# Two gate blocks of a latent-attention layer as seven products of halves, and where 32 modulation sums stand

## The chip, the cores and the metric

One core of a Trainium2 chip runs the whole program. TensorE (PE) multiplies, VectorE (DVE), ScalarE (ACT) and GpSimd (POOL) do elementwise work, SyncE's queue (SP) and POOL issue transfers. The metric is the device time of one execution in microseconds (us); smaller is better.

## The reference, cut to what matters

Two layers over a sequence of 512 tokens with 2048 features, all in fp32. Each layer starts with a modulated norm; layer 1 (i = 0) mixes with retention, layer 2 (i = 1) with latent attention.

```python
for i in range(DEPTH):
    mod = (c_act @ ada_w[i] + ada_b[i])[:, None, :]
    shift, scale, gate = jnp.split(mod, 3, axis=-1)
    h = rmsnorm(x, norm_g[i]) * (1.0 + scale) + shift
    ...
    x = x + gate * y
```

```python
def mla_branch(h, ...):
    proj = h @ w_in
    cq, ckv, k_rope, g = jnp.split(proj, [512, 1024, 1088], axis=-1)
    q = rmsnorm(cq, q_norm_g) @ w_uq
    kv = rmsnorm(ckv, kv_norm_g) @ w_ukv
    ...
    o = causal_block_attention(q, k, v)
    return (silu(g) * o) @ w_out
```

The gate g has 2048 columns; the kernel makes it in four blocks of 512. The row of `mod` that is called `gate` takes, for layer 2, 32 sums over 128 x 1024 pieces of `ada_w` (16 for each half of the features); the kernel's names for the halves are (1, 2, 0) and (1, 2, 1).

## The kernel before, in words

Every fp32 product is three products of the fp32r format: each operand is split into a high part (an ACT cast) and a low part (a DVE subtraction), and PE does high by high, high by low, low by high (L163 to L165). So each weight tile of 128 x 1024 costs an ACT cast and a DVE subtraction before PE can use it.

The program up to attention is a list of steps. The main loop takes them in order; for each step it issues the loads on SP, prepares the weights of this step and of `lead` steps ahead, writes the small pieces hung on the step (`beside`), the matmuls, then the modulation sums whose loads the step before asked for (as many as its `rows`), and asks for the next step's. A modulation sum is a DVE instruction with an accumulated output (L1076) on a tile that SP loads into one of two buffers. Each engine works through its own instructions strictly in the order written, PE's weight loads aside.

In order of time: layer 1's projections, some of them in **narrow blocks** (`narrow_steps`: seven products of halves in place of eight, 14 steps of 24 matmuls with 256 columns, so 336 in a block; the program there is L857 to L970); three retention rounds n = 0, 1, 2, in which the output projection (`round_steps`, L1374) is multiplied while the heads of the next pair go through rotation, scores and values; a last round with the block's tail; then layer 2's gate blocks 0 and 1, the query and key/value latents ("c", up to 1625.72 us), **gate blocks 2 and 3** (to 1716.37 us; `g2_steps`: 8 steps of 24 matmuls with 512 columns each, no product saved), and the attention cycles, one for each pair of heads, with the output projection behind.

A narrow block's step names: `b11` (four tiles of one quarter), then for each of two pairs `o`, `a` and `b` steps; `prepare_a` and `prepare_b` first make sums of raw weight halves on DVE (L931 to L935). Its end steps combine seven PSUM banks m1 to m7 into four results: ACT copies, DVE additions (`after_o`, `after_a`, `after_b`).

During gate blocks 2 and 3 three other things happen: the latents are normalised (`latent_norm`, `latent_scale`), each is transposed on PE by 16 transposes (`latent_transposes`, L1755) and split into parts for the attention products (`latent_parts`: qT, kvT); and DVE does the 32 sums of (1, 2, *), two per step.

Of the kernel before, what the change touches and what calls it, by code (L numbers as in the profile page):

```python
# [49 lines left out]
def hybrid_trunk_kernel(  # L50
# [47 lines left out]
    def k4(name, dt=F32R):  # L98
        return base.tile([P, 2, T], dt, tag="k4", bufs=8, name=name)
# [10 lines left out]
    def aux(name):  # L110
        return psum.tile([P, T], F32, tag="aux", bufs=4, name=name)
# [323 lines left out]
    def queued(fn, *args):  # L435
        with behind(A_, V_, T_, S_):
            return fn(*args)
# [848 lines left out]
    def light(block, which, n=1):  # L1286

        for i in which:
            block[i].rows = n
# [126 lines left out]
    for n in range(3):  # L1416
        block = []
        cols = range(4) if n % 2 == 0 else range(3, -1, -1)
        for r, after in zip(cols, [*cols[1:], None]):
            block += round_steps(n, r, go_on(n, r, after))  # L1420
        heads += [retention(2 * n + 2 + i, big) for i in range(2)]
        light(block, (0, 2, 3, 4, 6, 7, 10, 11, 12, 14, 15))
        light(block, (0, 3, 7), 2)
        steps += block


# [152 lines left out]
    for b in range(4):  # L1579
        block[2].beside["multiply"].append(lambda b=b: write_whole(b))  # L1580
        block[3].beside["form"].append(lambda b=b: ACT.copy(o1_banks[3, 2, b], x1_block(b, 2)))
        block[5].beside["form"].append(lambda b=b: seed(3, 0, b))
        block[0].beside["load"].append(lambda b=b: load_residual(3, b, "vr"))
        block[2].beside["load"].append(lambda b=b: load_residual(2, b, "ld"))
        block[5].beside["load"].append(lambda b=b: load_residual(0, b, "vr"))
        block[9].beside["load"].append(lambda b=b: load_residual(1, b, "ld"))
    steps += block
    for h, pieces in enumerate(heads):
        place(pieces, steps, n_p + 16 * (h // 2) + 4 * (h % 2))
# [152 lines left out]
    def latent_scale(n):  # L1742
        for t in range(NT):
            r, v = latent[n, "r"][:, t : t + 1], latent[n][t]
            if t % 2:
                ACT.activation(v, v, AF.Identity, scale=r)
            else:
                DVE.tensor_scalar(out=v, in0=v, scalar1=r, scalar2=None, op0=ALU.mult)

    def latent_transposes(n):  # L1750
        latent[n, "ps"] = []
        for j in range(4):
            ps = aux(f"{n}T_{j}")
            for t in range(NT):
                PE.transpose(ps[:, t * P : (t + 1) * P], latent[n][t][:, j * P : (j + 1) * P], ident)  # L1755
            latent[n, "ps"].append(ps)

    def latent_parts(n, g_c):
        latent[n, "T"] = []
        for j, ps in enumerate(latent[n, "ps"]):  # L1760
            dst = k4(f"{n}T_{j}")
            ACT.activation(dst[:, 0, :], ps, AF.Identity, scale=g_c[:, j : j + 1])
            DVE.scalar_tensor_tensor(
                out=dst[:, 1, :], in0=ps, scalar=g_c[:, j : j + 1], in1=dst[:, 0, :].bitcast(F32),
                op0=ALU.mult, op1=ALU.subtract,
            )
            latent[n, "T"].append(dst)

    wc = w_mla_in[:, 0:1024].rearrange("k (j n) -> k j n", j=2)
    turns2 = turns(  # L1770
        ((lambda: pools["l2"], "bw", 2), (lambda: base, "raw", 3)),
# [3 lines left out]
        "c", lambda kt, j: wc[kt * P : (kt + 1) * P, j, :], lambda n, u, b: form(h2, sums2, n, u, b), *turns2,  # L1775
        latent_rows, lambda second, u: 0,
    )
    g23 = g2_steps(2, rows=lambda u: 2) + g2_steps(3, rows=lambda u: 2)
    for i, n, g_c in ((0, "q", qn_s), (1, "kv", kvn_c)):
        g23[i].beside["form"].append(lambda n=n: latent_norm(n))  # L1780
        g23[i + 1].beside["form"].append(lambda n=n: latent_scale(n))
        g23[2 + 2 * i].beside["multiply"].append(lambda n=n: latent_transposes(n))
        g23[3 + 2 * i].beside["form"].append(lambda n=n, g_c=g_c: latent_parts(n, g_c))
    steps += g23


# [120 lines left out]
    def attend(h):  # L1907
# [72 lines left out]

        return scores, exps, lambda: (queued(reciprocals), queued(normalise)), transposes, split_pt, load_gate, values, result

    def attention_step(pr):

        nx = pr + 1
        here = [attend(2 * pr + s) for s in range(2)] if pr >= 0 else ()
        both = heads2[nx] = {}
        units_ahead()
        if here:
            (sc0, ex0, no0, tr0, sp0, lg0, va0, re0), (sc1, ex1, no1, tr1, sp1, lg1, va1, re1) = here  # L1990
            queued(lg0)
            queued(lg1)
        low = next_unit("ukv")
        if here:
            for i in range(NT):
                queued(sc0, i)
            for i in range(NT):
                queued(ex0, i)
        low()
        if here:  # L2000
            no0()
        queued(uq_products, nx, 2)
        if here:
            for i in range(NT):
                queued(sc1, i)
            for i in range(NT):
                queued(ex1, i)
        t1 = queued(rope_own, both["uq", 2], f"qr_{nx}")
        low = next_unit("ukv") if here else lambda: None
        if here:  # L2010
            no1()
        low()
        for b in range(2):
            queued(uq_products, nx, b)
        sw = queued(rope_swap, both["uq", 2], f"qr_{nx}")
# [12 lines left out]
        queued(rope_lows, t1, both["qr"])  # L2028
        for b in range(2):
            queued(uk_products, nx, b)  # L2030
            low = queued(part_pair, nx, "uk", b)
            low_w = next_unit("uq")
            queued(low)
            low_w()
        if here:
            queued(va0)
            queued(re0)
            queued(tr1)
            for low in [queued(sp1, j) for j in range(3)]:
# [19 lines left out]
    def all_rows():  # L2059
        pieces = [(0, 2, 0), (0, 2, 1), (1, 0, 0)]  # L2060
        yield from later_modulation(pieces, load_c(lpp, "bm", 2), lpp, [("bw", 2)])
        while "l1" not in pools:
            yield None
        l1p = pools["l1"]
        yield from later_modulation([(1, 0, 1), (1, 1, 0), (1, 1, 1)], load_c(l1p, "odd1", 2), l1p, [("odd0", 2)])
        while "l2" not in pools:
            yield None
        yield from later_modulation(
            [(1, 2, n) for n in range(2)], load_c(base, "k4b", 4), pools["l2"], [("bw", 2), ("pt", 4), ("pt", 4)]
        )  # L2070

    later = all_rows()
    loads = [load for step in steps for load, _ in step.units]
# [301 lines left out]
```

## Time and profile before

| | |
|---|---|
| Three runs | 2162.42, 2164.13, 2165.01 us (median 2164.13) |
| Profiled execution | 2164.31 us, its span 2162.5 us |
| PE busy | 2137.0 us, 99% |
| DVE busy | 1641.6 us, 76% |
| ACT busy | 1044.6 us, 48% |
| POOL busy | 103.7 us, 5% |
| DMA | 440.34 MB, mean 204 GB/s |

The profile is of one execution. Times of the trace run from the start of the span. A row of the timeline gives an instruction's start and its length; DVE, ACT and PE instructions overlap at their ends, so the step from one start to the next is a little shorter than a length. An idle time in square brackets is what the engine waited just before, with the engine and line that ended the wait.

### The profile page before, as it was taken

Reading aid. Unit: us, or ns where it says so; the run is one execution under the profiler, and the core shown is the slowest. Engines: PE = TensorE matmul, PEld = TensorE weight load, DVE = VectorE, ACT = ScalarE, POOL = GpSimd, SP = SyncE. Lnnn points to the kernel's source line nnn. Section 1 sums busy time; section 2 is a strip of 40 time slices with the busy share of each in tenths; the row PEclk is TensorE's granted clock in tenths of the full one; section 3 lists DMA queues with packets and bytes.
Section 4 is the critical chain, followed back from the end, with each engine's and each line's share of the span. In section 5 each row is a group of like instructions: output and inputs, shape, how many; then the busy total and the mean of one; then the engine's idle time right before and its main releaser. Section 6 shows DMA issues by size and latency. Waiting matters only on the chain.

```text
span 2162.5 us, 29040 instructions
## 1 busy us (share of the span) xinstructions
PE 2137.0 (99%) x10782; PEld 1814.0 (84%) x10782; DVE 1641.6 (76%) x2411; ACT 1044.6 (48%) x1581; POOL 103.7 (5%) x175
## 2 busy tenths in 40 slices
PE   8999999999999999999999999999999999999997
PEld 6888989898987887888888888898888899888887
DVE  8988878888889788666777777767967777775545
ACT  6767344444444444434344544434444365664443
POOL 0010000010000000000000000010001000000000
PEclk9999999999999999999999999999999999999999
DMA  9975575766668777765646565753458633335333
GB/s 385 384 251 197 191 252 193 232 212 226 223 211 285 243 243 268 233 201 171 222 158 238 170 215 199 245 174 98 169 174 323 239 97 93 101 97 185 113 104 130
DMA packets 204848, 440.34 MB, mean 204 GB/s; under 512 B 19185, under 2 KB 56081, under 8 KB 200865
## 3 DMA queue, kind: packets, MB, share of 16 engines
q1 hardware_dynamic: 192640, 399.57, 55.1%
q0 software_dynamic: 11920, 38.91, 4.7%
q8 instruction: 84, 1.38, 0.3%
q14 instruction: 58, 0.48, 0.1%
q10 hardware_dynamic: 146, 0.01, 0.0%
HBM read 395.42 MB, written 43.00 MB: 203 GB/s over the span
## 4 chain that ended last, share of the span: by engine, by line
PE 85%; DVE 6%; issue 4%; ACT 2%; DMA 2%; POOL 1%; SPq 0%; DVEq 0%; POOLq 0%; ACTq 0%
PE o L1374 14%; PE qk_m L870 7%; PE o L2241 4%; PE x L775 2%; PE y L775 2%; PE y L776 2%; PE y L774 2%; PE x L776 2%; PE x L774 2%; PE s L775 2%; PE s L776 2%; PE s L774 2%; PE qk L412 2%; PE o L165 2%; PE o L164 2%
## 5 line engine op out<-in xcount | busy, mean ns | idle before, releaser
L1374 PE MATMUL o<-o_h,o_whi 128*128 128x512 f32 (+1 forms) x496 | 192.2, 388 | 0.0
L1374 PE MATMUL o<-o_h,o_wlo 128*128 128x512 f32 (+1 forms) x496 | 191.4, 386 | 0.0
L1374 PE MATMUL o<-o_l,o_whi 128*128 128x512 f32 (+1 forms) x496 | 191.3, 386 | 0.0
L138 DVE TENSOR_TENSOR o_wlo<-o_r,o_whi 128x1024 fp32r<-128x1024 f32 x61 | 74.6, 1223 | 49.5 <-ACT o_whi L137 49.4
L1374 PEld LDWEIGHTS o<-o_h,o_wlo 128*128 128x128 f32 x496 | 93.2, 188 | 18.7
L1374 PEld LDWEIGHTS o<-o_h,o_whi 128*128 128x128 f32 x496 | 93.2, 188 | 18.3
L1374 PEld LDWEIGHTS o<-o_l,o_whi 128*128 128x128 f32 x496 | 93.2, 188 | 18.2
L163 PE MATMUL g<-h,g_h 128*128 128x512 f32 x232 | 90.6, 390 | 0.3 <-ACT g_h L137 0.3
L164 PE MATMUL g<-h,g_h 128*128 128x512 f32 x232 | 90.3, 389 | 0.0
L165 PE MATMUL g<-h,g_l 128*128 128x512 f32 x232 | 89.8, 389 | 0.0
L163 PE MATMUL qk<-hT,qk_h 128*128 128x512 f32 x192 | 74.9, 390 | 0.0
L164 PE MATMUL qk<-hT,qk_h 128*128 128x512 f32 x192 | 74.7, 389 | 0.0
L165 PE MATMUL qk<-hT,qk_l 128*128 128x512 f32 x192 | 74.6, 389 | 0.0
L137 ACT CAST o_whi<-o_r 128x1024 fp32r<-128x1024 f32 x61 | 63.5, 1051 | 20.2 <-issue 10.2
L1076 DVE SCALAR_TENSOR_TENSOR mod<-mod,c_odd 128x1024 f32<-128x1024 f32 x48 | 58.5, 1220 | 17.4 <-DMA mod<-in_ada_t_dram 17.4
L353 DVE SCALAR_TENSOR_TENSOR aw<-aw,c_all 128x2048 f32<-128x2048 f32 x30 | 67.5, 2285 | 0.0
L138 DVE TENSOR_TENSOR o_w_lo<-o_w_raw,o_w_hi 128x1024 fp32r<-128x1024 f32 x32 | 39.0, 1220 | 36.9 <-ACT o_w_hi L137 36.9
L138 DVE TENSOR_TENSOR o_l<-o_in,o_h 128x1024 fp32r<-128x1024 f32 x24 | 29.3, 1223 | 48.2 <-ACT o_h L137 48.2
L1076 DVE SCALAR_TENSOR_TENSOR mod<-mod,c_bm 128x1024 f32<-128x1024 f32 x48 | 58.5, 1219 | 4.8 <-DMA mod<-in_ada_t_dram 4.8
L2241 PE MATMUL o<-o_l,o_w_hi 128*128 128x512 f32 (+1 forms) x160 | 55.5, 347 | 0.9 <-DVE o_l L138 0.9
L2241 PE MATMUL o<-o_h,o_w_hi 128*128 128x512 f32 (+1 forms) x160 | 55.7, 348 | 0.2 <-ACT o_h L137 0.2
L2241 PE MATMUL o<-o_h,o_w_lo 128*128 128x512 f32 (+1 forms) x160 | 55.4, 346 | 0.0
(1308 smaller groups left out, 6625.8 us busy)
## 6 DMA issues: line engine op xcount, KB each, us to landing
mod<-in_ada_t_dram SPq DMA_DIRECT2D x128, 512.0 KB, 5.9
o_r<-in_ret_w_out_dram SPq DMA_DIRECT2D x64, 512.0 KB, 4.9
aw<-in_ada_t_dram SPq DMA_DIRECT2D x30, 1024.0 KB, 7.5
g_r<-in_mla_w_in_dram SPq DMA_DIRECT2D x32, 512.0 KB, 4.5
o_w_raw<-in_mla_w_out_dram SPq DMA_DIRECT2D x32, 512.0 KB, 3.8
qk_r<-in_ret_w_in_dram SPq DMA_DIRECT2D x48, 256.0 KB, 3.1
qk_o_r<-in_ret_w_in_dram SPq DMA_DIRECT2D x32, 256.0 KB, 4.3
qk_r<-qk_d SPq DMA_DIRECT2D x32, 256.0 KB, 6.4
```

The source lines that it names most:

```text
L138: DVE.tensor_sub(lo, src, hi.bitcast(F32))
L163: PE.matmul(o, lhs[0], rhs[0], start=first and not seeded, stop=False, skip_group_check=seeded)
L164: PE.matmul(o, lhs[0], rhs[1], start=False, stop=False, skip_group_check=seeded)
L165: return PE.matmul(o, lhs[1], rhs[0], start=False, stop=last, skip_group_check=seeded)
L353: DVE.scalar_tensor_tensor(out=aw, in0=aw, scalar=1.0, in1=c_all, op0=ALU.mult, op1=ALU.mult, accum_out=col,)
L774: PE.matmul(banks[b], a[0], w[0], start=first, stop=False, skip_group_check=True)
L775: PE.matmul(banks[b], a[0], w[1], start=False, stop=False, skip_group_check=True)
L776: PE.matmul(banks[b], a[1], w[0], start=False, stop=True, skip_group_check=True)
L870: PE.matmul(o, p, q, start=first and b + k == 0, stop=k == 2, skip_group_check=True)
L1076: DVE.scalar_tensor_tensor(out=aw, in0=aw, scalar=1.0, in1=silu_c[j], op0=ALU.mult, op1=ALU.mult, accum_out=mc[:, j, b : b + 1],)
L1374: PE.matmul(o, w[i][:, ki, c0 + b * P : c0 + (b + 1) * P], a[j], start=first and i + j == 0, stop=last and i == 1, skip_group_check=True,)
L2241: PE.matmul(banks2[b][:, cols], w[0][i][:, 0, b * P : (b + 1) * P], o2_moving(w, u, cols)[j], start=u + i + j == 0, stop=u == KD - 1 and i ...
```

## The change

Gate blocks 2 and 3 are made by `narrow_steps`, as layer 1's narrow blocks are; `keep` applies Silu in place on ACT and stores through POOL. Their raw tiles come from tags that the loads of that stretch used (`gate_raw`, five turns over two pools). The steps prepare two ahead.

The query latent is transposed one block of 128 at a time in gate block 3's steps (`latent_turn`, `latent_part`), through a single PSUM bank; the key/value latent's 16 transposes and its parts move into the first attention step (`attention_step(-1)`), behind the products that are called `uq_2`.

Of the 32 sums, the 16 of (1, 2, 0) go into the retention rounds: step 8 of each gets one where it had none, steps 10, 11 and 14 two where they had one, so 18 per round instead of 14; steps 8 to 11 of the last block get one each. The 16 of (1, 2, 1) become `row_turn`, two in each attention cycle, with one weight tile `gate_w` for all: each turn is followed on SP's queue by the load of the next tile (`row_load`), which has to wait for that turn.

```diff
-        light(block, (0, 2, 3, 4, 6, 7, 10, 11, 12, 14, 15))
-        light(block, (0, 3, 7), 2)
+        light(block, (0, 2, 3, 4, 6, 7, 8, 10, 11, 12, 14, 15))
+        light(block, (0, 3, 7, 10, 11, 14), 2)
...
+    light(block, (8, 9, 10, 11))
...
-    g23 = g2_steps(2, rows=lambda u: 2) + g2_steps(3, rows=lambda u: 2)
-    for i, n, g_c in ((0, "q", qn_s), (1, "kv", kvn_c)):
...
+    def gate_raw(shape, name):
+        raw_turn[0] += 1
+        pool, tag, bufs = ((pools["l2"], "bw", 2), (base, "raw", 3))[(raw_turn[0] % 5) in (2, 4, 0)]
+        return pool.tile(shape, F32, tag=tag, bufs=bufs, name=f"{name}_r")
...
+        def keep(half, j, c):
+            ACT.activation(c, c, AF.Silu)
...
+        return narrow_steps(
+            f"g2_{gi}", lambda e, j, u0, n: w[e, j][:, u0 : u0 + n, :], lambda n, u: form_half(h2, sums2, n, u),
+            gate_raw, turns2[1], keep,
+        )
...
+    for gi in (2, 3):
+        block = narrow_gates(gi)
+        for step in block[: 13 if gi == 3 else 14]:
+            step.lead = 2
+        for i in (3, 10):
+            block[i].ahead = 2
+        g23 += block
...
-        g23[i + 1].beside["form"].append(lambda n=n: latent_scale(n))
-        g23[2 + 2 * i].beside["multiply"].append(lambda n=n: latent_transposes(n))
-        g23[3 + 2 * i].beside["form"].append(lambda n=n, g_c=g_c: latent_parts(n, g_c))
+        g23[i + 2].beside["form"].append(lambda n=n: latent_scale(n))
+    for j in range(4):
+        g23[14 + 5 + 2 * j].beside["multiply"].append(lambda j=j: latent_turn("q", j))
+        g23[14 + 6 + 2 * j].beside["form"].append(lambda j=j: latent_part("q", qn_s, j, latent["q", "bank"]))
...
+    def row_turn():
...
+        DVE.scalar_tensor_tensor(
+            out=gate_rows["w"], in0=gate_rows["w"], scalar=1.0, in1=gate_rows["c"], op0=ALU.mult, op1=ALU.mult,
+            accum_out=gate_rows["m"][:, j, b : b + 1],
+        )
...
+            row_load(n + 1)
...
+        if pr < 0:
+            for j in range(4):
+                latent["kv", j] = aux(f"kvT_{j}")
+                for t in range(NT):
+                    queued(PE.transpose, latent["kv", j][:, t * P : (t + 1) * P], latent["kv"][t][:, j * P : (j + 1) * P], ident)
...
         low()
+        queued(row_turn)
...
+            if b:
+                queued(row_turn)
             queued(uk_products, nx, b)
```

DVE's order in retention round n = 1, from step 8 to step 9, before (`o_1_1_2_wlo` is the low part of the output weights, `v_0` to `v_3` those of the values that PE multiplies in this step):

```order
L138 TENSOR_TENSOR qk_1_0p<-rope_1_0_t_10407,qk_1_0p 128x512
L138 TENSOR_TENSOR o_1_1_2_wlo_10449<-o_1_1_2_r,o_1_1_2_whi_10448 128x1024
L138 TENSOR_TENSOR v_0_10452<-v_4_r,v_0_10452 128x512
L138 TENSOR_TENSOR v_1_10455<-v_4_r,v_1_10455 128x512
L138 TENSOR_TENSOR v_2_10458<-v_4_r,v_2_10458 128x512
L138 TENSOR_TENSOR v_3_10461<-v_4_r,v_3_10461 128x512
```

and after:

```order
L138 TENSOR_TENSOR qk_1_0p<-rope_1_0_t_10421,qk_1_0p 128x512
L1076 SCALAR_TENSOR_TENSOR mod_1_0_51_10373,mod_1_0_c<-mod_1_0_51_10373,c_odd_8946 128x1024
L138 TENSOR_TENSOR o_1_1_2_wlo_10464<-o_1_1_2_r,o_1_1_2_whi_10463 128x1024
L138 TENSOR_TENSOR v_0_10467<-v_4_r,v_0_10467 128x512
L138 TENSOR_TENSOR v_1_10470<-v_4_r,v_1_10470 128x512
L138 TENSOR_TENSOR v_2_10473<-v_4_r,v_2_10473 128x512
L138 TENSOR_TENSOR v_3_10476<-v_4_r,v_3_10476 128x512
```

One modulation sum now stands ahead of the low part of the weights and of the values.

DVE's order where gate block 2 ends and gate block 3 begins, after (`g_2_m` are PSUM banks of block 2, `g_3_..._l` low parts of block 3's weights; L931 to L935 make the raw sums for the `a` and `b` steps). Before, this place held one low part and two modulation sums for each step:

```order
L875 TENSOR_TENSOR g_3_b_0_l<-g_3_b_0_r,g_3_b_0_h 128x1024
L954 TENSOR_TENSOR g_2_p_14786<-g_2_m_14469,g_2_p_14786 128x512
L955 TENSOR_TENSOR g_2_v<-g_2_p_14786,g_2_p_14822 128x512
L956 TENSOR_TENSOR g_2_v<-g_2_m_14439,g_2_v 128x512
L875 TENSOR_TENSOR g_3_o_l<-g_3_o_r,g_3_o_h 128x1024
L962 TENSOR_TENSOR g_2_p_14786<-g_2_m_14494,g_2_p_14786 128x512
L964 TENSOR_TENSOR g_2_c_14859<-g_2_m_14507,g_2_p_14786 128x512
L966 TENSOR_TENSOR g_2_p_14822<-g_2_p_14786,g_2_p_14822 128x512
L931 TENSOR_TENSOR g_3_o_r<-g_3_o_r,g_3_a_r 128x512
L932 TENSOR_TENSOR g_3_a_r<-g_3_a_r,g_3_b_0_r 128x512
L933 TENSOR_TENSOR g_3_a_r<-g_3_o_r,g_3_b_0_r 128x512
L935 TENSOR_TENSOR g_3_o_r<-g_3_o_r,g_3_a_r 128x512
```

and ACT's order at the same place (L1772 is the Silu in `keep`, L874 the high part of a weight tile):

```order
L1772 ACTIVATE g_2_c_14788<-g_2_c_14788 128x512
L874 CAST g_3_b_0_h<-g_3_b_0_r 128x1024
L953 COPY g_2_p_14822<-g_2_m_14456 128x512
L1772 ACTIVATE g_2_v<-g_2_v 128x512
L874 CAST g_3_o_h<-g_3_o_r 128x1024
L1772 ACTIVATE g_2_c_14859<-g_2_c_14859 128x512
L1772 ACTIVATE g_2_p_14822<-g_2_p_14822 128x512
L874 CAST g_3_a_h<-g_3_a_r 128x1024
```

The combining additions of block 2 now stand between block 3's low parts, and three Silus between its casts.

DVE's order at the beginning of attention, before (kvT's parts were written while gate blocks 2 and 3 ran):

```order
L1076 SCALAR_TENSOR_TENSOR mod_2_1_70_14993,mod_2_1_c<-mod_2_1_70_14993,c_k4b_14297 128x1024
L1076 SCALAR_TENSOR_TENSOR mod_2_1_71_14995,mod_2_1_c<-mod_2_1_71_14995,c_k4b_14298 128x1024
L1087 TENSOR_TENSOR mod_2_1_s<-mod_2_1_c 128x8
L1090 TENSOR_TENSOR gate_c_95<-mod_2_1_s,vcol 128x8
L138 TENSOR_TENSOR kr<-kr_f,kr 128x512
L1793 TENSOR_TENSOR ukv_1_1_15054<-ukv_1_r,ukv_1_0_15053 128x1024
L1804 TENSOR_TENSOR qr_t_15072<-uq_2_15059,cos_12815 128x512
L1808 TENSOR_TENSOR qr_sw<-qr_sw,sin_12817 128x512
L1809 TENSOR_TENSOR qr_t_15072<-qr_t_15072,qr_sw 128x512
```

and after:

```order
L962 TENSOR_TENSOR g_3_p_15284<-g_3_m_14972,g_3_p_15284 128x512
L964 TENSOR_TENSOR g_3_c_15356<-g_3_m_14985,g_3_p_15284 128x512
L966 TENSOR_TENSOR g_3_p_15323<-g_3_p_15284,g_3_p_15323 128x512
L138 TENSOR_TENSOR kr<-kr_f,kr 128x512
L1825 TENSOR_TENSOR ukv_1_1_15378<-ukv_1_r,ukv_1_0_15377 128x1024
L1836 TENSOR_TENSOR qr_t_15416<-uq_2_15383,cos_12867 128x512
L2038 SCALAR_TENSOR_TENSOR gate_w,mod_2_1_c<-gate_w,gate_c 128x1024
L1794 SCALAR_TENSOR_TENSOR kvT_15446<-kvT_15396,vcol,kvT_15446 128x512
L1794 SCALAR_TENSOR_TENSOR kvT_15449<-kvT_15401,vcol,kvT_15449 128x512
L1794 SCALAR_TENSOR_TENSOR kvT_15452<-kvT_15406,vcol,kvT_15452 128x512
L1794 SCALAR_TENSOR_TENSOR kvT_15455<-kvT_15411,vcol,kvT_15455 128x512
L1840 TENSOR_TENSOR qr_sw<-qr_sw,sin_12869 128x512
```

The end of gate block 3, a first row turn (L2038) and the four parts of kvT now stand here, ahead of `uk_0`, whose products read kvT.

## Rows read from the trace of the kernel before

**Rows 1.** the page: busy time of the engines, share of the span, instructions

```profile
PE 2137.0 (99%) x10782; PEld 1814.0 (84%) x10782; DVE 1641.6 (76%) x2411; ACT 1044.6 (48%) x1581; POOL 103.7 (5%) x175
```

**Rows 2.** waits of TensorE's weight loads: us in total, times, longest us

```profile
PEld y L164 <- DVE v L138: 1.3, 3, 0.6
```

**Rows 3.** windows, TensorE: us, busy (instructions), granted clock, DMA share, GB/s

```profile
1625.72:1716.37 90.65, 90.65 (x418) 1.00 0.82 303
1499.83:1543.36 43.53, 43.23 (x191) 1.00 0.40 133
```

**Rows 4.** windows, TensorE, the four narrow blocks; columns as in 3

```profile
203.35:243.49 40.14, 40.14 (x338) 1.00 0.61 207
320.65:361.12 40.47, 40.46 (x337) 1.00 0.58 195
...
sum 161.43, PE 161.41; mean PE 40.35
```

**Rows 5.** one line's instructions: the latent transposes, ns min/median/max

```profile
L1755 PE MATMUL kvT<-ident,kv x16: 270/272/273, 1654.7 to 1656.4; 128*128 128x128 f32 x16
```

**Rows 6.** timeline, TensorE, second narrow block: start, us, instruction

```profile
326.39 0.64 PE L870 MATMUL qk_m<-sums,qk_a_h 128*128 128x256 f32 x4
327.04 0.39 PE L870 MATMUL qk_m<-sums,qk_a_l 128*128 128x256 f32 x1
```

**Rows 7.** timeline, VectorE, second narrow block and its end

```profile
325.76 1.23 DVE L875 TENSOR_TENSOR qk_a_l<-qk_a_r,qk_a_h 128x1024 fp32r<-128x1024 f32 x1 [0.45 <-ACT qk_a_h L874]
...
359.32 0.68 DVE L954 TENSOR_TENSOR qk_p<-qk_m,qk_p 128x512 f32<-128x512 f32 x1
...
362.81 0.68 DVE L966 TENSOR_TENSOR qk_p<-qk_p,qk_p 128x512 f32<-128x512 f32 x1
```

**Rows 8.** timeline, ScalarE, end of the second narrow block

```profile
357.10 1.05 ACT L808 CAST vg_00o_h<-vg_00o_r 128x1024 fp32r<-128x1024 f32 x1 [0.40 <-PE qk_m L870]
358.05 0.58 ACT L953 COPY qk_p<-qk_m 128x512 f32<-128x512 f32 x1
```

**Rows 9.** groups, ScalarE, in 1625 to 1716: busy us, mean ns

```profile
L1739 ACT ACTIVATE q_sq<-q 128x512 f32<-128x512 f32 x4 | 2.5, 621 | 0.0
```

**Rows 10.** timeline, VectorE, rounds n=0 and n=1

```profile
1078.99 2.49 DVE L138 TENSOR_TENSOR v<-v_r,v 128x512 fp32r<-128x512 f32 x4
...
1190.84 1.23 DVE L138 TENSOR_TENSOR o_wlo<-o_r,o_whi 128x1024 fp32r<-128x1024 f32 x1 [0.26 <-ACT o_whi L137]
1191.98 2.50 DVE L138 TENSOR_TENSOR v<-v_r,v 128x512 fp32r<-128x512 f32 x4
```

**Rows 11.** timeline, TensorE, the same places

```profile
1079.88 0.40 PE L164 MATMUL y<-v,sT 128*128 128x512 f32 x1
...
1192.72 0.50 PE L164 MATMUL y<-v,sT 128*128 128x512 f32 x1
```

**Rows 12.** the page: modulation sums of layer 1's part, idle before and releaser

```profile
L1076 DVE SCALAR_TENSOR_TENSOR mod<-mod,c_odd 128x1024 f32<-128x1024 f32 x48 | 58.5, 1220 | 17.4 <-DMA mod<-in_ada_t_dram 17.4
```

**Rows 13.** timeline, VectorE, rounds n=1 and the last block

```profile
1155.42 1.23 DVE L1076 SCALAR_TENSOR_TENSOR mod<-mod,c_odd 128x1024 f32<-128x1024 f32 x1 [2.44 <-DMA mod<-in_ada_t_dram]
...
1216.38 1.22 DVE L138 TENSOR_TENSOR o_wlo<-o_r,o_whi 128x1024 fp32r<-128x1024 f32 x1 [4.11 <-ACT o_whi L137]
...
1426.95 0.48 DVE L1340 SCALAR_TENSOR_TENSOR x<-o,gate_c,o_xr 128x256 f32<-128x256 f32 x1 [4.92 <-PE o L1374]
```

**Rows 14.** the page: loads, KB each, median us to landing

```profile
mod<-in_ada_t_dram SPq DMA_DIRECT2D x128, 512.0 KB, 5.9
...
ukv_r<-in_mla_w_ukv_dram SPq DMA_DIRECT2D x16, 512.0 KB, 3.6
```

**Rows 15.** timeline, VectorE, one attention cycle

```profile
1780.04 1.22 DVE L1793 TENSOR_TENSOR ukv<-ukv_r,ukv 128x1024 fp32r<-128x1024 f32 x1
...
1788.17 1.02 DVE L1793 TENSOR_TENSOR uq<-uq_r,uq 128x256 fp32r<-128x256 f32 x2
...
1795.28 0.69 DVE L1793 TENSOR_TENSOR v<-uv,v 128x512 fp32r<-128x512 f32 x1 [1.90 <-ACT v L1792]
```

More of the change, by code (lines that the diff above doesn't have):

```diff
@@ L1748, in latent_scale @@
                 DVE.tensor_scalar(out=v, in0=v, scalar1=r, scalar2=None, op0=ALU.mult)
[L1750 to L1767, printed above, removed]
     wc = w_mla_in[:, 0:1024].rearrange("k (j n) -> k j n", j=2)
@@ L1777, in hybrid_trunk_kernel, with narrow_gates @@
     )
-    g23 = g2_steps(2, rows=lambda u: 2) + g2_steps(3, rows=lambda u: 2)
-    for i, n, g_c in ((0, "q", qn_s), (1, "kv", kvn_c)):
+    raw_turn = [0]
+    def gate_raw(shape, name):
+        raw_turn[0] += 1
+        pool, tag, bufs = ((pools["l2"], "bw", 2), (base, "raw", 3))[(raw_turn[0] % 5) in (2, 4, 0)]
+        return pool.tile(shape, F32, tag=tag, bufs=bufs, name=f"{name}_r")
+    def narrow_gates(gi):
+        w = w_mla_in[:, 1088 + gi * 512 : 1600 + gi * 512].rearrange("(u e p) (j n) -> e j p u n", e=2, p=P, j=2)
+        def keep(half, j, c):
+            ACT.activation(c, c, AF.Silu)
+            r0 = (gi * 4 + 2 * j) * P
+            POOL.dma_start(
+                sg2_d[r0 : r0 + 2 * P, half * H : (half + 1) * H].rearrange("(b p) t -> p b t", p=P),
+                c.rearrange("p (b t) -> p b t", b=2),
+            )
[3 more added lines that the diff above has]
+        )
@@ new lines, in latent_turn, with latent_part @@
+    def latent_turn(n, j):
+        if j == 0:
+            latent[n, "bank"] = aux(f"{n}T")
+        ps = latent[n, "bank"]
+        for t in range(NT):
+            PE.transpose(ps[:, t * P : (t + 1) * P], latent[n][t][:, j * P : (j + 1) * P], ident)
+    def latent_part(n, g_c, j, ps):
+        dst = k4(f"{n}T_{j}")
+        ACT.activation(dst[:, 0, :], ps, AF.Identity, scale=g_c[:, j : j + 1])
+        DVE.scalar_tensor_tensor(
+            out=dst[:, 1, :], in0=ps, scalar=g_c[:, j : j + 1], in1=dst[:, 0, :].bitcast(F32),
+            op0=ALU.mult, op1=ALU.subtract,
+        )
+        latent[n, "T"].append(dst)
@@ L1780, in hybrid_trunk_kernel @@
+    steps[-1].lead = 2
+    latent["q", "T"], latent["kv", "T"] = [], []
+    g23 = []
+    for gi in (2, 3):
[5 more added lines that the diff above has]
+        g23 += block
+    for i, n in ((1, "q"), (4, "kv")):
         g23[i].beside["form"].append(lambda n=n: latent_norm(n))
-        g23[i + 1].beside["form"].append(lambda n=n: latent_scale(n))
-        g23[2 + 2 * i].beside["multiply"].append(lambda n=n: latent_transposes(n))
@@ L1981, in attend, with row_load @@
         return scores, exps, lambda: (queued(reciprocals), queued(normalise)), transposes, split_pt, load_gate, values, result
+    gate_rows = {}
+    def row_load(n):
+        j, b = n // 8, n % 8
+        if n == 0:
+            gate_rows["c"], gate_rows["w"] = (l2_tile("bw", 2, f"gate_{k}", (P, 2, T)) for k in "cw")
+            gate_rows["m"] = base.tile([P, 2, 8], F32, tag="mod_c", bufs=2, name="mod_1_2_1_c")
+        if b == 0:
+            nc.sync.dma_start(
+                gate_rows["c"].rearrange("p a n -> p (a n)"),
+                c_d[0:1, j * 1024 : (j + 1) * 1024].rearrange("o n -> (o n)").partition_broadcast(P),
+            )
+        r0 = 2 * D + (8 + b) * P
+        nc.sync.dma_start(
+            gate_rows["w"], ada_t[1, r0 : r0 + P, j * 1024 : (j + 1) * 1024].rearrange("p (a n) -> p a n", a=2)
+        )
+    def row_turn():
+        n = gate_rows["n"]
+        if n == 16:
+            return
+        gate_rows["n"] = n + 1
+        j, b = n // 8, n % 8
+        DVE.scalar_tensor_tensor(
+            out=gate_rows["w"], in0=gate_rows["w"], scalar=1.0, in1=gate_rows["c"], op0=ALU.mult, op1=ALU.mult,
+            accum_out=gate_rows["m"][:, j, b : b + 1],
+        )
+        if n == 15:
+            use_modulation(1, 2, 1, gate_rows["m"])
+        else:
+            row_load(n + 1)
     def attention_step(pr):
+        if pr < 0:
+            gate_rows["n"] = 0
+            queued(row_load, 0)
         nx = pr + 1
@@ L2002, in attention_step @@
         queued(uq_products, nx, 2)
+        if pr < 0:
+            for j in range(4):
+                latent["kv", j] = aux(f"kvT_{j}")
+                for t in range(NT):
+                    queued(PE.transpose, latent["kv", j][:, t * P : (t + 1) * P], latent["kv"][t][:, j * P : (j + 1) * P], ident)
         if here:
@@ L2012, in attention_step @@
         low()
+        queued(row_turn)
         for b in range(2):
             queued(uq_products, nx, b)
+        if pr < 0:
+            for j in range(4):
+                queued(latent_part, "kv", kvn_c, j, latent["kv", j])
         sw = queued(rope_swap, both["uq", 2], f"qr_{nx}")
@@ L2064, in all_rows @@
         l1p = pools["l1"]
[L2065 to L2070, printed above, removed]
+        yield from later_modulation([(1, 0, 1), (1, 1, 0), (1, 1, 1), (1, 2, 0)], load_c(l1p, "odd1", 2), l1p, [("odd0", 2)])
     later = all_rows()
```

## The prediction

> **What bounds the kernel now.** I read the busy times first. TensorE is busy for 2137.0 of 2162.5 us [rows 1], so only about 25 us of the span are not TensorE's. The reader is to see two things in that row: nothing but fewer or shorter matmuls can bring much, and every stall that a change puts in front of TensorE counts in full. VectorE's 76% is a mean over stages that differ much, so it says nothing of a single place. I then took the waits of TensorE's weight loads, which show where TensorE already arrives before its operands: one of them, for the low part of the values in the retention rounds, comes three times, up to 0.6 us each [rows 2]. After that I cut the span into windows: the two gate blocks take 90.65 us, a plain gate block without transposes in it 43.53 us for its 192 matmuls [rows 3], and the four narrow blocks 161.43 us together, 40.36 each [rows 4]. Last I read timelines at the places where the change moves work. The granted clock is 1.00 in the windows of both kinds of block, so prices can be carried from one to the other.
>
> **The gain.** The plain block gives 43.53 / 192 = 0.2267 us per matmul of 512 columns [rows 3], the narrow block 40.36 / 336 = 0.1201 us per matmul of 256 [rows 4]. The stretch holds 32 transposes besides: 16 run from 1654.7 to 1656.4, 1.66 us with the last one's step, and 32 cost 3.3 us [rows 5]. They stay in the program, 16 of them in attention. So 90.65 − 3.3 = 87.3 us of products become 2 × 40.36 = 80.7 us: **−6.6 us**, if nothing is late. One in eight of the products is saved, but a half-wide matmul costs 0.120 and not 0.113 us.
>
> TensorE's weight loads run for 1814.0 us beside 2137.0 us of matmuls [rows 1], so they overlap nearly everywhere. The Trainium skill ("TensorE: Matmul & The Clock Gate", sections "Back-to-back issue gap" and "LDWEIGHTS (loading the stationary operand)") prices a lone matmul at N/2.4 + 2.5 ns, a weight load of 128 columns at 107 ns, and says that in a stream both set the pace; a rule that speaks against halves, since 256 columns leave hardly any time beyond the weight load. By its lone-matmul formula the two blocks would fall from 82.9 to 73.4 us, an estimate of 9.5 us of gain; these rows, at 0.2267 and 0.120, are above it at both widths and agree with the pace set by both.
>
> **Retention rounds.** Twelve more sums go into the three rounds, at 1.22 us each [rows 12]. The one at step 8 is the expensive one. There VectorE does the low part of the weights at 1190.84 after 0.26 us of idle time, then the values' low parts from 1191.98 [rows 10]. An instruction of that width lasts 0.68 [rows 7], so the first of those is done at 1192.66, and TensorE takes it at 1192.72 [rows 11]: it was waiting for it. In round 0 the same low part is done at 1078.99 + 0.68 = 1079.67 and is taken at 1079.88, 0.2 us to spare [rows 10, 11]. The sum enters ahead of both, with a step of 1.14 us (the step from 1190.84 to 1191.98 of an instruction of that size); 0.26 is absorbed by the idle time, so the values come 0.88 later. TensorE loses 0.88 − 0.2 in round 0 and 0.88 in the others, as round 2 is among the three waits: **+2.4 us**, bounds 0 (if VectorE makes the time good before it gets there) and 4.
>
> The second sums of steps 10, 11 and 14 stand before idle stretches: behind step 11's sum VectorE waits 4.11 us for ScalarE [rows 13]. A pair's second load can start only when the sum before it has freed a buffer, and such a sum has waited 2.44 us for its transfer [rows 13]; 2.44 + 1.14 is under 4.11. I take 0. If the transfer is slower than that, some tenths per round come on top, which the bound of 4 holds. The last block's four sums stand in a stretch with idle times up to 4.92 us [rows 13]: 0.
>
> **Gate block 2.** In a narrow block the first `a` step is late already: its high parts start at 326.39, four of them would be through at 326.87, the low part starts at 327.04 [rows 6], while VectorE made that low part from 325.76 [rows 7]. That wait, about 0.3 us, is the difference between 40.14 and 40.47 [rows 4] and so is in the mean. Here ScalarE has the latents' squares besides, 4 × 0.62 us for each latent [rows 9], in front of the high parts of an `o` step, and the second b11 tile takes its buffer late. A step lasts 24 × 0.12 = 2.9 us and asks ScalarE for one cast of 1.05 us [rows 8], which hides most of it: **+0.6 us**, bounds 0 and 1.4.
>
> **The joint of block 2 and block 3.** Call block 3's start B. The layer 1 narrow blocks are followed by another kind of block, so no row shows this joint; I build it from the rows of one end. VectorE's first combining addition of bank m6 comes at 359.32, 1.8 us before that block's end at 361.12, the last at 362.81, 1.7 us behind it [rows 7]; in the new order m6 can be taken at B − 2.9, one step ahead, so `v` is ready at about B − 0.7 after three additions with their hand-overs. From there it is one chain through two engines in strict order: Silu of `v` on ScalarE 0.58 and the cast of block 3's `o` 1.05 [rows 8], ready at B + 1.0; its low part 1.23, B + 2.2; three additions that end block 2 and three raw sums of the `a` step, six times 0.66, B + 6.2; the cast 1.05 with its hand-over, B + 7.3; the low part 1.23 [rows 7], B + 8.6. TensorE wants the low part after 48 matmuls of b11 and `o` and four of `a`, 52 × 0.12 = B + 6.2. It stands still for 2.4 us, 0.3 of which the mean of rows 4 has: **+2.1 us**, bounds 0 (the additions could be through before the cast of `o`) and 3.
>
> **The beginning of attention.** `uk_0` reads kvT, which was ready long before. Now TensorE goes through uq_2, the transposes, uq_0 and uq_1 first: 36 × 0.2267 + 1.66 = 9.8 us. VectorE ends block 3 about 2.3 us after its end (1.7 + 0.6), then kr, ukv_1, qr_t, the row turn and the first kvT: 0.6 + 1.14 + 0.6 + 1.14 + 0.65 = 4.1 (0.6 to 0.7 for the narrow ones, 1.14 for the wide), at 6.4. That leaves 3.4 us, but uq_1 must wait for a buffer that block 3's last low part frees and ukv_1 for the next, and such a load takes 3.6 us [rows 14]; what goes beyond 3.4 is late, hand-overs included. **+0.6 us**, bounds 0 and 2.
>
> **The attention cycles.** Two turns of 1.14 us in each. They shift VectorE's later work, but it idles 1.90 us before the values' low part [rows 15], so the turns are absorbed: **0**. The transfer is the open point: with one buffer the load starts at the end of the first turn, which stands behind the low part of 1780.04, so at about 1782.3, and must land before the second, behind the one of 1788.17, so at about 1789.7: 7.4 us. The median landing of such a load is 5.9 us [rows 14]. On SP's queue the next weight loads stand behind each `gate_w` load; the buffers they need are freed by low parts that VectorE makes behind the turn, so they lose little. Bounds 0 and 4 us over the cycles. Removing 32 sums from the gate blocks gives nothing: TensorE did not wait there (busy 90.65 of 90.65) [rows 3].
>
> **The sum**, against the profiled execution: 2164.31 − 6.6 + 2.4 + 0.6 + 2.1 + 0.6 + 0 = **2163.4 us**. That execution lies 0.18 us above the median of the runs, 2164.13, so I leave it as it is.
>
> **Rivals.** (a) *The stalls are hidden*: the chains slide because VectorE is ahead of TensorE where I have it level. For it speaks that VectorE gets rid of 32 sums in the gate stretch. Against it: the round's wait stands in the trace [rows 2]. With 0 to 2.2 us of losses left: 2157.7 to 2159.9. (b) *A half-wide matmul costs half*: 672 × 0.1133 = 76.2 us, a gain of 11.1, 2158.9 after the same losses. Four blocks speak against it [rows 4]. The skill's lone-matmul formula would put it between, at 2160.5. (c) *The gate tile is late, slower*: the load of `gate_w` lands after its turn is due, VectorE stands with the low parts behind it, and TensorE with them. The 1.90 us of idle time [rows 15] cover a landing up to 7.4 + 1.9 = 9.3 us; each us beyond that costs 1 us in each of about seven cycles. The 5.1 us from the forecast to 2168.5 are reached at 10.0 us; at 10.4 it is 2163.4 + 7.7 = 2171. The median of 5.9 [rows 14] speaks against it. (d) *Sums in the rounds stand in the way more often*: if six of the nine second sums cost 1.14 us too, 2170. The idle stretches of rows 13 speak against it.
>
> **How the numbers follow.** 0.2%, or 4.3 us, is about what a measurement of this kernel can tell from no change. The forecast, with its terms within their bounds, 0.63 (its own range 2160 to 2166); (a) 0.21; (b) 0.04; (c) 0.06; (d) 0.06. So faster by over 0.2% (below 2159.8) has (a) and (b) and a little of the forecast's low end, 0.26; slower (above 2168.5) has (c) and (d) but for their near ends, 0.10; within 0.2%, 0.64. The range reaches half into (a) and to the start of (c) and (d): 2158.6 to 2167.4.
>
> **What would show it.** Right: two blocks of about 40.9 and 42.5 us between "c" and attention; the low part of the values in each round 0.7 to 0.9 us later against TensorE; a wait for block 3's first `a` of about 2 us; no wait of VectorE on `gate_w` that reaches TensorE. Wrong: block 3 without that wait (2 us less), rounds of unchanged length (2.4 less), or waits on the values in every attention cycle (several us more). A gate stretch above 84 us would say that the price of a narrow matmul did not carry over.

## The result, and the profile after

The changed kernel takes 2166.68 us (median of 20 runs, 2164.78 to 2170.6), the kernel before 2163.66 us (20 runs, 2162.18 to 2165.69): a ratio of 1.0015 with a 95% interval of 1.0009 to 1.0022. It is 3.0 us slower. Forecast were 2163.4 us for a profiled execution of 2164.31, so 0.9 us faster. The time lies inside the stated range, the sign is wrong.

TensorE has less to do, as intended: 11070 matmuls in place of 10782, many of them half as wide. But its share of the span fell. The page, busy time of the engines:

```profile
PE 2132.3 (98%) x11070; PEld 1823.2 (84%) x11070; DVE 1684.1 (78%) x2469; ACT 1057.9 (49%) x1597; POOL 103.4 (5%) x175
```

Busy time fell by 4.7 us against [rows 1] while the span grew from 2162.5 to 2164.9 us, so about 7 us of new waits are to be found. TensorE's waits by line (us in total, times, longest):

```profile
PE y L164 <- DVE v L138: 2.3, 3, 0.9
PE a L163 <- DVE o L2010: 2.2, 1, 2.2
PE g_m L870 <- ACT g_a_h L874: 1.6, 1, 1.6
...
PE a L163 <- ACT p L1965: 0.8, 1, 0.8
...
PE g_m L870 <- DVE g_a_l L875: 0.5, 1, 0.5
```

The first was there before, as the weight loads' wait of [rows 2], and smaller; the joint of the gate blocks (`g_m`) was expected; the two waits of `a`, attention's scores, were not (the one for `p` was 0.2 us before). The windows say what each stage is worth. TensorE in the changed kernel: the rounds; gate block 2, gate block 3 with the query latent's 16 transposes, the beginning of attention; then the last attention cycle that prepares a next pair of heads, from the start of its value products on, and the stretch behind it up to the output products (us, busy (instructions), granted clock, DMA share, GB/s):

```profile
1026.04:1366.82 340.78, 337.64 (x1575) 1.00 0.63 220
1628.11:1669.02 40.91, 40.90 (x338) 1.00 0.38 110
1669.02:1713.65 44.63, 42.46 (x354) 1.00 0.46 138
1713.65:1729.05 15.40, 15.40 (x79) 1.00 0.51 165
...
1917.63:1951.87 34.24, 32.03 (x196) 1.00 0.45 141
1951.87:1982.11 30.24, 29.43 (x184) 1.00 0.73 244
```

The same stages in the kernel before, where rows 3 do not have them (the two gate blocks are there, 90.65 us):

```profile
1026.10:1364.47 338.37, 337.34 (x1576) 1.00 0.60 204
1716.37:1729.96 13.59, 13.59 (x61) 1.00 0.34 119
...
1918.55:1950.31 31.76, 31.76 (x195) 1.00 0.41 127
1950.31:1979.78 29.47, 29.29 (x184) 1.00 0.72 238
```

The rounds lose 340.78 − 338.37 = 2.4 us. The gate blocks and the beginning of attention gain 90.65 + 13.59 − (40.91 + 44.63 + 15.40) = 3.3 us. The last attention cycle has 34.24 us, which is 2.5 more, and the stretch behind it 0.8 more. The cycles ahead of it are as long as before: from the value products of the first to those of the last but one it is 1917.63 − 1729.05 = 188.58 us now and 1918.55 − 1729.96 = 188.59 then, by the ends of these windows. The rest of the program differs by less than 0.1 us in every stage. That is 2.4 − 3.3 + 2.5 + 0.8 = 2.4 us, as much as the spans differ by.

In the last cycle the wait is for a weight of the next stage. ScalarE in the changed kernel (timeline: start, us, instruction, and in brackets the idle time before it):

```profile
1926.20 1.05 ACT L137 CAST o_w_hi<-o_w_raw 128x1024 fp32r<-128x1024 f32 x1 [4.84 <-DMA o_w_raw<-in_mla_w_out_dram]
...
1927.28 1.23 DVE L138 TENSOR_TENSOR o_w_lo<-o_w_raw,o_w_hi 128x1024 fp32r<-128x1024 f32 x1 [5.19 <-ACT o_w_hi L137]
1928.42 0.68 DVE L1825 TENSOR_TENSOR v<-uv,v 128x512 fp32r<-128x512 f32 x1
1929.02 0.68 DVE L2010 TENSOR_TENSOR o<-o,sg 128x512 f32<-128x512 f32 x1
```

The cast of the first output weight, `o_w_hi`, stands on ScalarE between the two casts of `v`, and waits 4.84 us for its load; the second low part of `v`, and `o`, which TensorE waits for, stand behind it. In the kernel before this cast stood one place further ahead, before both casts of `v`:

```profile
1923.61 1.05 ACT L137 CAST o_w_hi<-o_w_raw 128x1024 fp32r<-128x1024 f32 x1 [4.08 <-DMA o_w_raw<-in_mla_w_out_dram]
```

It waited there too, for 4.08 us, and TensorE lost nothing: it began 5.1 us after the start of the cycle's value products. Now it begins 8.6 us after it. SP's queue, first after, then before, from the gate tiles of the two heads (`sg`, in full `sg_12` and `sg_13`) on:

```profile
1917.28 2.03 SPq L1996 DMA_DIRECT2D sg<-sg_d  x2
1919.42 9.50 SPq L144 DMA_DIRECT2D o_w_raw<-in_mla_w_out_dram  x2
```

```profile
1916.67 0.46 SPq L1964 DMA_DIRECT2D sg<-sg_d  x1
1918.13 0.37 SPq L144 DMA_DIRECT2D o_w_raw<-in_mla_w_out_dram  x1
1918.73 0.34 SPq L1964 DMA_DIRECT2D sg<-sg_d  x1
```

Before, the queue had one gate tile (`sg`), `o_w_raw`, then the other gate tile. After, both gate tiles come first, and the second has to wait for its buffer (2.03 us for the two), so `o_w_raw` goes out at 1919.42. Counted from the start of the cycle's value products (1918.55 before, 1917.63 after) that is 0.4 us ahead of it then and 1.8 us behind it now, so 2.2 us later. From its issue to the start of the cast the load took 5.5 us then and 6.8 now; both together are the 3.5 us by which the cast is late.

### The profile page after: what moved, and what is told of

It reads as the page before. It is cut to its first block, busy times and chain, and to the rows that moved or that the text cites. A ratio compares the mean times of both kernels' runs of the same rounds, so it can differ in the third digit from the quotient of the medians.

```text
span 2164.9 us, 29773 instructions
## 1 busy us (share of the span) xinstructions
PE 2132.3 (98%) x11070; PEld 1823.2 (84%) x11070; DVE 1684.1 (78%) x2469; ACT 1057.9 (49%) x1597; POOL 103.4 (5%) x175
## 4 chain that ended last, share of the span: by engine, by line
PE 82%; DVE 8%; issue 4%; ACT 3%; DMA 2%; POOL 0%; SPq 0%; DVEq 0%; POOLq 0%; ACTq 0%
PE o L1374 13%; PE qk_m L870 7%; PE o L2314 4%; PE g_m L870 3%; PE x L775 2%; PE y L775 2%; PE y L776 2%; PE y L774 2%; PE x L776 2%; PE x L774 2%; PE s L775 2%; PE s L776 2%; PE s L774 2%; PE qk L412 2%; PE qk L165 2%
## 5 line engine op out<-in xcount | busy, mean ns | idle before, releaser
L138 DVE TENSOR_TENSOR o_wlo<-o_r,o_whi 128x1024 fp32r<-128x1024 f32 x61 | 74.6, 1224 | 36.8 <-ACT o_whi L137 36.7
L1076 DVE SCALAR_TENSOR_TENSOR mod<-mod,c_odd 128x1024 f32<-128x1024 f32 x64 | 77.4, 1221 | 17.6 <-DMA mod<-in_ada_t_dram 17.6
L137 ACT CAST o_h<-o_in 128x1024 fp32r<-128x1024 f32 x24 | 25.2, 1048 | 57.5 <-PE o L164 46.7
L137 ACT CAST o_w_hi<-o_w_raw 128x1024 fp32r<-128x1024 f32 x32 | 33.4, 1047 | 39.7 <-PE o L2314 33.8
L138 DVE TENSOR_TENSOR qk_l<-qk_r,qk_h 128x1024 fp32r<-128x1024 f32 x24 | 29.1, 1224 | 30.2 <-ACT qk_h L137 30.0
```

The source lines that it names most:

```text
L137: ACT.copy(hi, src)
L138: DVE.tensor_sub(lo, src, hi.bitcast(F32))
L1076: DVE.scalar_tensor_tensor(out=aw, in0=aw, scalar=1.0, in1=silu_c[j], op0=ALU.mult, op1=ALU.mult, accum_out=mc[:, j, b : b + 1],)
```

## The experiments

Each is an edit of the changed kernel, unless it says otherwise. The medians are of 8 to 11 runs; the kernel before, beside them on the same chip, had 2163.8 to 2164.0 us. One such median says less than a window of its trace, since the runs of one kernel spread over 3 to 7 us.

**Queue order alone.** In the last cycle the second gate tile (`lg1` asks for it) is asked for later, so that the first output weight, `o_w_0`, stands ahead of it.

```diff
-            queued(lg1)
+            if pr < NPR - 2:
+                queued(lg1)
...
+        if pr == NPR - 2:
+            queued(lg1)
         both["qr"] = big(f"qr_{nx}")
```

> The changed kernel with one load moved: in the last attention cycle the gate tile sg_13 is asked for later, so that on SP's queue the first output weight o_w_0 stands ahead of it again, as before the change. All sums, turns and gate blocks as changed. Theory A (the queue: o_w_0's load stood behind sg_13's wait for a buffer, its cast on ScalarE stands ahead of the values' cast): the last cycle goes from 34.2 us back to 31.8 to 32.1, 2.1 to 2.5 us less in all, about 2164.3. Rival B (the two turns on VectorE in that cycle delay the values): the last cycle stays at 34.2 us and the time at 2166.7.

Median 2166.77 us; five of its eleven runs lie at 2162.4 to 2164.9, six at 2166.8 to 2167.5. The windows of its last cycle, of the stretch behind it, and two from within that stretch:

```profile
1918.07:1949.95 31.88, 31.88 (x196) 1.00 0.46 154
1949.95:1982.66 32.71, 31.06 (x183) 0.95 0.66 226
...
1963.00:1966.00 3.00, 2.18 (x9) 0.69 0.88 339
1966.00:1968.00 2.00, 2.00 (x7) 0.61 0.85 271
```

The cycle is back at 31.88 us with both turns still in it: theory A for that cycle, and B is out. But in this execution the stretch behind it takes 32.71 us, 3.2 more than before the change, so nothing is won. About half of that is waiting: TensorE stands for 32.71 − 31.06 = 1.65 us, against 0.2 before. The scores wait for exponentials, and ahead of these on ScalarE stands a cast that waits for its load:

```profile
1960.39 1.05 ACT L137 CAST o_h<-o_in 128x1024 fp32r<-128x1024 f32 x1 [3.83 <-DMA o_in<-o_d]
```

The other half is the clock: TensorE is busy for 31.06 us with what took 29.29 before, and its granted clock was 0.69 and 0.61 in the two stretches shown, the first of which holds the second of these waits.

**No turn in the last cycle.** Three turns in two early cycles, so that the sixteen are through before the last. SP's queue then comes out in the order of before by itself.

```diff
             queued(queued(part_values, nx, j))
+        if pr in (0, 1):
+            queued(row_turn)
```

> The changed kernel with three row turns in each of the first two attention cycles after the opening one, so that the last cycle has none. SP's order in the last cycle comes out as before the change, with o_w_0 ahead of sg_13, and VectorE is free of turns there. Theory A: last cycle 31.76 us, 2.5 us less in all, about 2164.2; the third turns cost nothing in their cycles. Rival B (turns on VectorE): the same in the last cycle, but the two cycles with three turns get longer, by 1 us or more each.

Median 2164.08 us, 2.6 less.

```profile
1917.94:1949.69 31.75, 31.75 (x196) 1.00 0.42 130
1949.69:1979.17 29.48, 29.30 (x183) 1.00 0.70 240
```

Both stretches are as before the change (31.76 and 29.47), and the cycles with three turns took 31.76 us each like all others. So a turn in those cycles costs nothing; where the last ones stood, they moved SP's queue.

**The rounds' sum at step 13 in place of step 8.**

```diff
-        light(block, (0, 2, 3, 4, 6, 7, 8, 10, 11, 12, 14, 15))
+        light(block, (0, 2, 3, 4, 6, 7, 10, 11, 12, 13, 14, 15))
```

> The changed kernel with the rounds' new sum at step 13 in place of step 8; the count per round stays at 18. Theory (step 8's sum stands ahead of the values' low parts that TensorE waits for): each round is shorter by 0.8 us, 2.4 us in all, about 2164.3, since VectorE idles 1.8 us near step 13. Rival (any four more sums in a round cost this much, as VectorE is behind as a whole): the wait appears elsewhere in the round and the time stays at 2166 to 2167.

Median 2165.2 us. The window of the three rounds:

```profile
1025.42:1363.90 338.48, 337.46 (x1575) 1.00 0.64 221
```

338.48 us against 338.37 before the change and 340.78 with step 8: the whole 2.3 us are the one sum per round that stood ahead of the values' low parts. The count of sums is the same, so the rival falls. The median is only 1.5 us less; this kernel's runs spread the most, over 7.1 us.

**The sums moved, the gate blocks plain.** The kernel before with the sums where the change puts them.

```diff
-    g23 = g2_steps(2, rows=lambda u: 2) + g2_steps(3, rows=lambda u: 2)
+    g23 = g2_steps(2) + g2_steps(3)
```

> The kernel before with only the sums moved: plain gate blocks 2 and 3 and the latents' transposes as before, the 16 sums of (1, 2, 0) in the rounds and the last block, the 16 of (1, 2, 1) as turns in attention. If the narrow blocks give 3.3 us net here, as the two traces say, and the sums cost 2.4 in the rounds and 2.5 in the last cycle, this is 2163.7 + 2.4 + 2.5 = 2168.6 with the last cycle as in the changed kernel, or 2166.1 if SP's order comes out as before. Rival (the narrow blocks give nothing, the loss is theirs): 2163.7.

Median 2169.64 us. Its gate blocks with the beginning of attention, and its last cycle:

```profile
1627.52:1731.77 104.25, 104.25 (x477) 1.00 0.42 127
1920.34:1954.17 33.83, 31.99 (x195) 1.00 0.44 145
```

The gate stretch is that of before, 104.25 us against 90.65 + 13.59 = 104.24: taking 32 sums out of it gives nothing. The last cycle loses 2.1 us, nearly as in the changed kernel, and the rounds have the same sums. So the narrow blocks are worth 3.3 us net, and moving the sums costs nearly 6. The time came out 1 us above the expectation. In the profiled execution the stretch behind the last cycle took 0.8 us more than before and the output 1.0, neither of which had been counted; what lengthened the output is open.

**The joint, first half: the Silu of `v` behind the cast of block 3's `o`.**

```diff
         def keep(half, j, c):
-            ACT.activation(c, c, AF.Silu)
+            if half == 0 and j == 1 and gi == 2:
+                held.append(c)
+                return
+            for c_ in held:
+                held.clear()
+                store(0, 1, c_)
+            store(half, j, c)
...
+        def store(half, j, c):
+            ACT.activation(c, c, AF.Silu)
```

> The changed kernel with one Silu of gate block 2 (that of v) put behind the cast of block 3's o on ScalarE. Theory (one chain over two engines, as the prediction built it): the cast of o no longer waits for v, o's low part follows v directly, and the first a of block 3 comes 1.6 us earlier; the wait of 2.5 us there falls to about 0.8 us, in all 1.6 us less. Rival (the loads of block 3's raw tiles set the a step, since the buffers come free late): the wait stays at 2.5 us.

Median 2165.7 us. The first window is gate block 3, the second the last attention cycle:

```profile
1668.69:1711.59 42.90, 42.38 (x354) 1.00 0.46 142
1915.57:1951.02 35.45, 33.61 (x195) 0.95 0.43 136
...
PE g_m L870 <- DVE g_a_l L875: 0.5, 1, 0.5
```

Block 3 takes 42.90 in place of 44.63 us, 1.7 less, and of its two waits only 0.5 us is left: the theory. The median fell by 1.0 us only. In the profiled execution the last cycle took 35.45 in place of 34.24 us, which has to do with the clock (last section).

**The joint, second half: block 2's last additions behind block 3's first `a`.**

```diff
+    late_end = g23[13].follow
+    g23[13].follow = lambda: None
+    g23[14].beside["form"].append(late_end)
```

> The changed kernel with block 2's three last combining additions (and their two Silus) put behind the raw sums and low part of block 3's first a. Theory: three times 0.66 us leave the chain and one more raw sum stays in it, so the wait of 2.5 us at the first a falls to 0.3 to 0.8 us, about 2 us less in all; the later additions cost nothing, as their banks are not needed before the next b step. Rival (loads): the wait stays.

Median 2166.73 us: nothing. Block 3 and TensorE's waits there:

```profile
1668.38:1713.20 44.82, 42.84 (x355) 1.00 0.44 135
...
PE g_m L870 <- ACT g_b_h L874: 0.9, 1, 0.9
...
PE g_m L870 <- DVE g_b_l L875: 0.5, 1, 0.5
```

The long wait of the `a` step is gone (0.5 us of it are left), and the `b` step behind it has waits of 0.9 and 0.5 us. They are for its cast, which now stands behind two Silus that wait for the late additions, and for its low part, which VectorE can begin only after that cast. 44.82 us against 44.63: the expectation that the later additions cost nothing was wrong.

**Together.** Three turns in two early cycles, step 13, both halves of the joint.

> The changed kernel with all that paid in the single trials: three turns in two early attention cycles and none in the last, the rounds' sum at step 13 in place of step 8, and the joint of blocks 2 and 3 with both reorderings. If the terms add (2.6 to 3.3 us in the last cycle and behind it, 2.3 in the rounds, 2.5 at the joint), 2166.7 - 7.8 = 2159 us, 0.2% below the kernel before. If they share a cover, 2160 to 2162.

Median 2159.2 us, ratio 0.9979 (0.9970 to 0.9987); a second time:

> The combination with the late end once more, beside the kernel without it on the same chip: 2159.2 as before; the two differ by less than 0.3 us if the late end does nothing.

2159.51 us, ratio 0.9980 (0.9971 to 0.9989). And without the second half of the joint:

> The previous combination without the late end of block 2: three turns in two early attention cycles and none in the last, the rounds' sum at step 13, and only the Silu of v behind the cast of block 3's o. If putting the end of block 2 later only moves the wait from the a step to the b step, as its single trial showed, this kernel is 0 to 0.3 us faster than the combination: about 2159. If the late end helps once the Silu is out of the way, it is 0.5 to 1 us slower: about 2160.

Median 2158.83 us, ratio 0.9977 (0.9968 to 0.9986), 5.2 us below the kernel before. Its rounds, its gate blocks with the beginning of attention, and its last cycle:

```profile
1025.39:1363.86 338.47, 337.46 (x1576) 1.00 0.65 221
1625.28:1724.48 99.20, 98.68 (x765) 1.00 0.43 133
1913.07:1944.83 31.76, 31.76 (x196) 1.00 0.41 129
```

The terms add: 338.47 and 31.76 are as before the change, and the gate stretch is 104.24 − 99.20 = 5.0 us shorter. The late end makes a difference of 0.7 us in the medians and 0.2 in the windows (99.41 with it), which the spread does not tell from nothing.

## Why the prediction was wrong, and where it was right

**The gain** was right. The price of a half-wide matmul carried over from layer 1's narrow blocks, and the plain blocks with moved sums put the net gain of the stretch at 3.3 us, which is the forecast's 6.6 − 0.6 − 2.1 − 0.6. That the sum agrees this well is luck in part: of its terms the joint was 0.5 us too small and the beginning of attention 0.45 too large (below). Block 2 has 40.91 us where 40.36 + 0.6 had been forecast, but not for the reason given: its `b11` and `o` steps take 2.87 to 2.93 us (2.85 to 2.88 in layer 1), and three of its four `a` steps take 3.05 to 3.14. The prediction's 40.9 and 42.5 us for the two blocks, and its sign of 84 us for the stretch, leave out the query latent's 16 transposes, 1.66 us, which the window of block 3 holds; without them the two blocks took 83.9 us.

The Trainium skill ("TensorE: Matmul & The Clock Gate", section "Back-to-back issue gap") was weighed there with its formula for a lone matmul and its sentence that weight loads and matmuls together set the pace. By the formula 336 matmuls of 256 columns would take 36.7 us, an estimate; block 2 took 40.91. The trace agrees with the sentence at this width: block 2's weight loads are busy for 40.38 of its 40.91 us, those of the plain block of [rows 3] for 35.48 of 43.53. The section's own sustained figure for 512 columns, 131 ns, does not fit: a matmul of the plain block took 227 ns, and the measurement decides.

**The rounds** were right, 2.4 us forecast and 2.4 measured. Round n = 1 after, at the place of [rows 10] and [rows 11]:

```profile
1191.24 1.22 DVE L1076 SCALAR_TENSOR_TENSOR mod<-mod,c_odd 128x1024 f32<-128x1024 f32 x1
...
1193.53 2.49 DVE L138 TENSOR_TENSOR v<-v_r,v 128x512 fp32r<-128x512 f32 x4
...
1194.26 0.50 PE L164 MATMUL y<-v,sT 128*128 128x512 f32 x1 [0.92 <-DVE v L138]
```

The sum stands ahead of `o_wlo` and the low part of `v`, and TensorE takes it as soon as it is there, 0.92 us after it could have. The second sums at steps 10, 11 and 14 cost nothing, as said: with step 8's gone the rounds are as long as before the change, and rival (d) is out.

**The joint** was right in its mechanism and 0.5 us small: block 3 without its transposes took 44.63 − 1.66 = 42.97 us, 2.6 above the mean narrow block, where 2.1 had been forecast. The chain came out nearly as it had been built from other rows: `o`'s low part ends at B + 2.4 (forecast 2.2), the cast of `a` starts at B + 6.5 (6.2), its low part is done at B + 8.8 (8.6), with B = 1669.02:

```profile
1670.22 1.23 DVE L875 TENSOR_TENSOR g_o_l<-g_o_r,g_o_h 128x1024 fp32r<-128x1024 f32 x1 [1.64 <-ACT g_o_h L874]
...
1676.56 1.23 DVE L875 TENSOR_TENSOR g_a_l<-g_a_r,g_a_h 128x1024 fp32r<-128x1024 f32 x1 [0.46 <-ACT g_a_h L874]
...
1668.62 0.63 ACT L1772 ACTIVATE g_v<-g_v 128x512 f32<-128x512 f32 x1 [2.98 <-DVE g_v L956]
1669.16 1.03 ACT L874 CAST g_o_h<-g_o_r 128x1024 fp32r<-128x1024 f32 x1
...
1675.48 1.04 ACT L874 CAST g_a_h<-g_a_r 128x1024 fp32r<-128x1024 f32 x1 [1.37 <-DVE g_a_r L933]
...
1676.58 0.74 PE L870 MATMUL g_m<-sums,g_a_h 128*128 128x256 f32 x4 [1.64 <-ACT g_a_h L874]
1677.84 0.39 PE L870 MATMUL g_m<-sums,g_a_l 128*128 128x256 f32 x1 [0.52 <-DVE g_a_l L875]
```

The Silu of `v` does stand ahead of the cast of `o` there, and taking it away gave 1.7 us, as the trial showed.

**The beginning of attention** was taken too high: 15.40 − 13.59 is 1.81, of which 1.66 are the transposes, so 0.15 us were lost and not 0.6.

**The attention cycles** are the step that failed. The text took 0 for them, with a bound of 4, and looked for the price in the landing of `gate_w` within its 7.4 us: rival (c). That never came up. No turn waited for its tile; the median landing was 4.9 us. The sentence that failed is the one on SP's queue, that the loads behind a `gate_w` load "lose little". It looked at the loads of a cycle like any other, where that holds to the hundredth. It did not look at the last cycle, in which the output weights' loads join the queue and a cast on ScalarE stands ahead of the values. There the order of three loads changed, and the price is 2.5 us in that cycle and 0.8 behind it, against a forecast gain of 0.9 in all. The bound of 4 us holds the 2.5, but by luck: it was set for transfers in cycles like any other. The order of SP's queue at the end of attention could be read before the run, beside the place of that cast; the listings in the section on the change show other places. That the changed order is the cause of the 2.5 us is shown from two sides: putting `o_w_0` ahead of `sg_13` again, with the turns in place, brings the cycle back to 31.88 us, and taking the turns out of that cycle restores order and time.

The 0.8 us of the stretch behind it have a cause of the same kind, as the trace reads. The cast `o_h`, ahead of the exponentials on ScalarE, waits for its load, first after, then before:

```profile
ACT o_h L137 <- DMA o_in<-o_d: 2.9, 1, 2.9
```

```profile
ACT o_h L137 <- DMA o_in<-o_d: 1.5, 1, 1.5
```

The loads of `o_in` go out from 1954.24 on, 2.4 us into the stretch, and from 1951.17 on before, 0.9 us into it. Ahead of them on SP's queue stand two output weights:

```profile
1951.34 1.90 SPq L144 DMA_DIRECT2D o_w_raw<-in_mla_w_out_dram  x2
```

Their buffers come free with two low parts on VectorE (1950.04 and 1951.25), and ahead of these stands the last turn (1948.90). By this chain a turn's own 1.22 us count in this place, by way of the queue. Without turns in the last cycle the loads go out 0.9 us into the stretch as before, and it loses nothing. No trial took one member of this chain away alone, so the chain is read and not shown.

## What to carry to other kernels

Where a kernel is bound by one engine for 99% of its span, work moved off a place that did not wait gains nothing, and what counts is what stands behind it where it goes: one sum of 1.22 us cost 0.8 us in each round, and the same sum five steps later nothing. A steady cycle says little about the last one: follow every queue into the stage where it meets the next stage's loads, and look for the cast that waits for such a load ahead of work on the path. And a chain over two engines can be shortened by moving one instruction of 0.6 us that nobody waits for, while moving the block's three last additions only put the wait one step further.

## What the hardware showed that had not been expected

A wait of TensorE can cost more than its length. In the profiled execution with the later Silu TensorE stood for 1.84 us in the last attention cycle, where it stands in the changed kernel too; then its granted clock was 0.50 for the next eight matmuls, that is the lower of its two levels, 1.2 GHz:

```profile
1925.15:1927.90 2.75, 0.91 (x4) 0.99 0.19 34
1927.95:1930.90 2.95, 2.95 (x8) 0.50 0.93 307
```

Eight matmuls of 512 columns took 2.95 us where 8 × 0.2267 = 1.8 would do, 1.1 us more. In the changed kernel's own profiled execution a wait of 2.2 us at the same place was not followed by it (1.00 in its window of the last cycle). So a wait in the same place costs 1 us more in one execution than in another. The first trial's two waits of 0.8 us, with granted clocks of 0.69 and 0.61 in the 5 us around and behind the second, are another case.

The mean granted clock of every run is on record, and it goes with the time. Of the changed kernel's 20 runs four had 0.996 and took 2168.5 us in the mean, eleven had 0.997 and took 2166.8, five had 0.998 and took 2166.0. The 77 runs of the kernel before beside the trials all had 0.997 or 0.998. So part of the changed kernel's wider spread, 5.8 us against 3.5, goes with the clock. Where in a run it fell, such a mean does not say; that it fell behind the new waits is likely from the traces and not shown.
